# First blocks in halves, u in pairs, another reader first on xm's bank, gate columns inside a z block, first output blocks by token tile

## The chip, the cores and the metric

The kernel runs on one core of a Trainium2 chip. PE is TensorE's matmul, PEld its weight load, DVE is VectorE, ACT is ScalarE, POOL is GpSimd, SP is SyncE, which only issues transfers here. The metric is the device time of one execution in microseconds, the median of several runs.

## The reference

Two layers on x of 256 tokens by 1024. Layer 0 mixes tokens with a gated MLP, layer 1 with an mLSTM; behind each stands a SwiGLU and a gated embedding.

```python
def gmlp_mixer(x, w_in, ln_g, ln_b, w_s, b_s, w_out):
    u, v = jnp.split(jax.nn.gelu(x @ w_in), 2, axis=-1)      # 3072 each
    v = layer_norm(v, ln_g, ln_b)
    sv = jnp.einsum('gts,bcsgd->bctgd', jnp.tril(w_s), v_in_groups) + b_s
    return (u * sv) @ w_out

def mlstm_mixer(x, ...):
    xm, z = jnp.split(x @ w_in, 2, axis=-1)                  # 2048 each
    xc = silu(causal_depthwise_conv(xm, conv_w, conv_b))     # 4 taps
    q, k, v = headwise_linear(xc, w_q), headwise_linear(xc, w_k), headwise_linear(xm, w_v)
    gates = concatenate([q, k, v]) @ w_gates + b_gates       # 4 heads, i and f
    h = mlstm_cell(q, k, v, i_pre, f_pre)                    # chunkwise, stabilised
    h = layer_norm(h, norm_g) + skip * xc
    return (h * silu(z)) @ w_out

def swiglu(x, w_gate, w_up, w_down):
    return (silu(x @ w_gate) * (x @ w_up)) @ w_down

for i in range(2):
    x = layer_norm(ALPHA * x + mixer_i(x), ln1_g[i], ln1_b[i])
    x = layer_norm(ALPHA * x + swiglu(x, ...), ln2_g[i], ln2_b[i])
    x = x + sigmoid(x @ ple_w_gate[i] + ple_b_gate[i]) * (p[i] @ ple_w_proj[i])
```

## The kernel before

All products are made in float32 out of two float32r parts: an operand is split into a high part (a cast, by ACT) and a low part (the difference, by DVE), and a product takes three matmuls: high by high, high by low, low by high. The weights come from memory as blocks of 128 by 1024 (512 KB, tile `raw`, four buffers) in the order of a plan, and `split` makes `w` of them. `ahead(loads, casts)` issues the loads of the next blocks on SP's queue and the splits of the next few; `weight(...)` calls it at each use. A raw buffer is free again when DVE has subtracted, and the next load waits for that. `EARLY` moves some blocks of a later stage up in the plan. The Tile scheduler sets the order of each engine's instructions from the order of the code and its own estimates; semaphores follow from the data.

The stages on PE, in the order of time:

- warm-up matmuls, then the six v columns (`vps`): tokens on the output's partitions, four blocks of weights each. x comes in four pieces of two K blocks (`xr`), the first of them as two transfers of ACT's queue; the first weight block comes and is split in halves of 512 columns (`HALF`), all others whole.
- the u blocks (`ups`, features on the partitions, 24 matmuls of 256 tokens), each followed by the spatial products (`svps`, `sv_block`) and, three blocks later, by the output matmuls (`acc`, 12 of 512). `us` is the Gelu of the bank.
- layer 0's SwiGLU, where g and u go in pairs: `feat_pair` multiplies the high weights by both parts of x at once (8 matmuls of 512 columns into two halves of one bank), then the low weights by the high part (8 of 256), and `pair_sum` adds the two halves (a copy by ACT, an addition by DVE).
- layer 1: z's first 512 features, then sixteen xm blocks (`xm_block`: the convolution from the bank, split of xm, Silu, split of xc), the q and v blocks two blocks later (`qv_block`, `qps`, `vps`), the scores a block after that (`s_block`), and z blocks 4 to 7 in between (`z_mm`).
- the gates: `gp` transposes the gate sums, DVE and ACT make the cumulative sums (`ai`, `G`, `ex`), `cp` transposes them back to columns, `gb` broadcasts G to all partitions for each head. z blocks 8 to 11 lie between.
- the heads: `pv_block(h)` makes `num` and `pd`, and a chain of small DVE and POOL operations gives the scale `hrs` and the offset `nb` with which ACT writes `hn`; then a z block each; `h_block(h)` transposes `hn` and makes four input blocks `h` of the output product.
- the output blocks `mo` (`Down.add`, tokens 0 to 127, then 128 to 255), layer 1's SwiGLU and embedding.

PSUM has eight banks, four of kind A (gp, cp, gb, num, acc) and four of kind B (vps, ups, svps, zps, tp, pg, pu); a tile waits for the readers of the bank's earlier tile.

Of the kernel before, what the change touches and what calls it, by code (L numbers as in the profile page):

```python
# [14 lines left out]
P = 128  # L15
D = 1024
S = 256
# [51 lines left out]
def paired(key):  # L69

    return key[0] in ("g", "u") and len(key) == 3 and key[-1] >= 4

# [60 lines left out]
def trunk(ctx, tc, a, out):  # L133
# [35 lines left out]
    def ahead(loads, casts):  # L169
        while at["load"] < min(len(plan), at["use"] + loads):  # L170
            ap = plan[at["load"]][1]
            n = ap.shape[-1]
            t = tl("raw", [P, n], name="raw")
            for c in HALF if at["load"] == 0 else [slice(0, n)]:
                sp.dma_start(t[:, c], ap[:, c])
            raws[at["load"]] = t
            at["load"] += 1
        while at["cast"] < min(len(plan), at["use"] + casts):
            i = at["cast"]
            key, raw = plan[i][0], raws.pop(i)  # L180
            n = raw.shape[-1]
            if key in WIDE:
                t = tl("b8", [P, 2, D], F32R, "w")
            else:


                first = ASIDE if stationary(key) and not paired(key) else 0
# [12 lines left out]
            wt[i] = t  # L200
            at["cast"] += 1
# [44 lines left out]

    def feat_from_x(ps, w):

        for k in range(KD):
            mm_feat(ps, w, slice(k * P, (k + 1) * P), xh[:, k, :], xl[:, k, :], k == 0, k == KD - 1)  # L250

# [96 lines left out]
    for i in range(4):  # L348
        t = tl("m2", [P, 2, S], name="xr")
        if i == 0:  # L350
            for k in range(2):
                act.dma_start(t[:, k, :], a["xT"][i, :, k, :])
        else:
            sp.dma_start(t, a["xT"][i])
        ahead(1 + i, int(i == 0))
        xr.append(t)
    make_identity(nc, ident)
# [288 lines left out]
    def mlstm(embed1):  # L646
# [41 lines left out]

        def z_mm(f):
            ps = bank("B", [P, S], "zps")  # L690
            feat_from_x(ps, weight("z", f, casts=2 if f > 10 else None))
            return f, ps
# [9 lines left out]
        def xm_block(f):  # L702
            ps = bank("B", [P, S], "xmps")
            feat_from_x(ps, weight("xm", f))
            y = tl("s", [P, S], name="conv")
            act.activation(y, ps, AF.Identity, bias=par[:, f, 4:5], scale=par[:, f, 3:4])
            for j in (1, 2, 3):
                dve.scalar_tensor_tensor(y[:, j:], ps[:, :S - j], par[:, f, 3 - j:4 - j], y[:, j:], ALU.mult, ALU.add)
# [85 lines left out]
        with tc.manual_schedule(engines={mybir.EngineType.Activation}):  # L794
            z8 = z_mm(8)
            gp = bank("A", [4, 2, S], "gp")
            for i in range(2):
                for t in range(2):
                    pe.transpose(gp[:, i, TOK[t]], gacc[:, t, 4 * i:4 * i + 4], ident)
            dve.tensor_scalar(fs, gp[:, 1, :], gbias[:, 1:2], None, ALU.add)  # L800
# [9 lines left out]
            z_copy(*z8)  # L810
            z = z_mm(9)
            cp = bank("A", [P, 4, 4], "cp")
            for i, src in enumerate((ai, ex)):
                for t in range(2):
                    pe.transpose(cp[:, 2 * i + t, :], src[:, TOK[t]], ident[:4, :4])
            dve.tensor_copy(cols[:, 0:2, :], cp[:, 0:2, :])

            dve.tensor_scalar(cols[:, 2:4, :], cp[:, 2:4, :], -88.0, None, ALU.max)
            for h in range(NH):
                gb = bank("A", [P, 2, P], "gb")  # L820
                pe.matmul(gb, selH[:, h, :], G, start=True, stop=True)
                if h in (0, 3):
                    z_copy(*z)
                    z = z_mm(10 if h == 0 else 11)
                gm = tl("s", [P, 2, P], name="gm")
# [13 lines left out]
            z_copy(*z)  # L839
            act.activation(sz[1][:, 0:4, :], sz[1][:, 0:4, :], AF.Silu)  # L840

        hn = []

        def pv_block(h):
# [18 lines left out]
            dve.tensor_tensor(dn, dn, pd[:, :, 0], ALU.max)  # L863
            dve.reciprocal(dn, dn)
            st = tl("c", [P, 2, 6], name="hst")
            mv = tl("c", [P, 2, 2], name="hmv")
# [137 lines left out]
```

## Time and profile before

| | us |
|---|---|
| median of 3 runs (837.59, 838.34, 840.28) | 838.34 |
| profiled execution | 837.17 |
| span of the profile | 835.4 |
| PE, DVE, ACT, POOL busy | 824.1, 608.8, 472.5, 158.4 |

The span is from the first to the last instruction on the core; the execution's time has 1.8 us more around it. The granted clock was 0.999. An engine's idle time counts only where PE ends up waiting for it.

### The profile page before, as it was taken

What the parts mean: (1) busy time and instruction counts of PE and PEld (TensorE: products, weight loads), DVE (VectorE), ACT (ScalarE), POOL (GpSimd) and SP (SyncE); (2) the same over time, 40 slices, a digit from 0 to 9 for tenths busy, and PEclk for the clock granted to TensorE, in tenths of its full rate; (3) what the DMA queues carried; (4) which work ended last, traced back from release to release, by engine and by line L of the source; (5) the groups of instructions that cost most, each with busy time, mean ns of one, the idle gap of its engine ahead of it and who ended that gap; (6) DMA issues with size and microseconds to landing.
All of it is one profiled execution on the core that took longest, in us unless ns stands there. A gap on an engine that the chain in (4) does not pass through costs nothing.

```text
span 835.4 us, 12743 instructions
## 1 busy us (share of the span) xinstructions
PE 824.1 (99%) x4727; PEld 719.6 (86%) x4727; DVE 608.8 (73%) x933; ACT 472.5 (57%) x803; POOL 158.4 (19%) x222
## 2 busy tenths in 40 slices
PE   8999999999999999999999999999999999999997
PEld 5889999998888888888889999898878888888886
DVE  6667996567856666578878998578886666677684
ACT  6556665555544555467347787685544555566522
POOL 1021654443100001800101655230010000000010
PEclk9999999999999999999999999999999999999999
DMA  8885465567286655588234444253646655577601
GB/s 299 294 304 178 143 196 192 177 196 243 102 290 202 188 191 193 164 261 265 80 134 165 140 140 154 95 193 121 209 166 243 206 190 193 187 244 259 202 0 52
DMA packets 44710, 155.55 MB, mean 186 GB/s; under 512 B 5224, under 2 KB 5992, under 8 KB 44648
## 3 DMA queue, kind: packets, MB, share of 16 engines
q1 hardware_dynamic: 44360, 154.47, 56.0%
q8 instruction: 37, 0.61, 0.3%
q10 hardware_dynamic: 288, 0.26, 0.1%
q14 instruction: 25, 0.20, 0.1%
HBM read 153.67 MB, written 1.05 MB: 185 GB/s over the span
## 4 chain that ended last, share of the span: by engine, by line
PE 63%; DVE 5%; DMA 3%; ACT 2%; issue 1%; POOL 1%; DVEq 0%; ACTq 0%; SPq 0%; POOLq 0%
PE pu L255 8%; PE pg L255 8%; PE acc L239 5%; PE acc L238 5%; PE acc L240 5%; PE pu L257 4%; PE pg L257 4%; PE gate L275 2%; PE gate L278 2%; PE gate L276 2%; PE first L275 2%; PE first L278 2%; PE first L276 2%; DVE w L152 2%; DMA raw<-in_ml_wo 1%; PE xmps L243 1%
## 5 line engine op out<-in xcount | busy, mean ns | idle before, releaser
L152 DVE TENSOR_TENSOR w<-raw,w 128x1024 fp32r<-128x1024 f32 (+1 forms) x277 | 337.2, 1225 | 108.6 <-ACT w L152 106.0
L152 ACT CAST w<-raw 128x1024 fp32r<-128x1024 f32 (+1 forms) x276 | 287.3, 1045 | 152.7 <-PE acc L240 50.7
L238 PE MATMUL acc<-w,h 128*128 128x512 f32 x336 | 132.0, 393 | 1.6 <-ACT hn L878 1.0
L239 PE MATMUL acc<-w,h 128*128 128x512 f32 x336 | 131.5, 391 | 0.0
L240 PE MATMUL acc<-w,h 128*128 128x512 f32 x336 | 130.8, 390 | 0.5 <-DVE w L152 0.5
L238 PEld LDWEIGHTS acc<-w,h 128*128 128x128 f32 x336 | 63.2, 188 | 14.5 <-ACT hn L878 1.4
L240 PEld LDWEIGHTS acc<-w,h 128*128 128x128 f32 x336 | 63.1, 188 | 14.5 <-DVE w L152 1.0
L239 PEld LDWEIGHTS acc<-w,h 128*128 128x128 f32 x336 | 63.2, 188 | 11.1 <-DVE h L152 0.3
L255 PE MATMUL pu<-xs,w 128*128 128x512 f32 x288 | 72.3, 393 | 0.0
L255 PE MATMUL pg<-xs,w 128*128 128x512 f32 x288 | 71.8, 391 | 0.0
L255 PEld LDWEIGHTS pg<-xs,w 128*128 128x128 f32 x288 | 53.8, 188 | 11.0
L307 POOL TENSOR_SCALAR ve<-mv 128x1 f32<-128x1 f32 x8 | 6.1, 758 | 294.8 <-DVE mv L327 290.5
L255 PEld LDWEIGHTS pu<-xs,w 128*128 128x128 f32 x288 | 51.5, 188 | 9.3
L244 PE MATMUL ups<-xs,w 128*128 128x256 f32 x192 | 53.7, 280 | 0.0
L243 PE MATMUL ups<-xs,w 128*128 128x256 f32 x192 | 53.6, 279 | 0.0
L245 PE MATMUL ups<-xs,w 128*128 128x256 f32 x192 | 53.6, 279 | 0.0
L442 POOL TENSOR_TENSOR sv<-sv,cf 128x256 f32<-128x256 f32 x24 | 31.1, 1298 | 67.8 <-ACT sv L441 64.0
L257 PEld LDWEIGHTS pg<-xs,w 128*128 128x128 f32 x288 | 38.9, 188 | 3.1
L257 PEld LDWEIGHTS pu<-xs,w 128*128 128x128 f32 x288 | 38.9, 188 | 3.1
L257 PE MATMUL pu<-xs,w 128*128 128x256 f32 x288 | 39.5, 279 | 0.0
L257 PE MATMUL pg<-xs,w 128*128 128x256 f32 x288 | 39.4, 279 | 0.0
L238 PE MATMUL vps<-w,xs 128*128 128x512 f32 x96 | 37.6, 392 | 1.5 <-ACT w L152 0.8
(240 smaller groups left out, 1675.7 us busy)
## 6 DMA issues: line engine op xcount, KB each, us to landing
raw<-in_ffn_g SPq DMA_DIRECT2D x44, 512.0 KB, 3.9
raw<-in_ffn_u SPq DMA_DIRECT2D x44, 512.0 KB, 4.0
raw<-in_ffn_d SPq DMA_DIRECT2D x44, 512.0 KB, 3.4
raw<-in_gm_u SPq DMA_DIRECT2D x24, 512.0 KB, 3.5
raw<-in_gm_wo SPq DMA_DIRECT2D x24, 512.0 KB, 3.4
raw<-in_gm_v SPq DMA_DIRECT2D x23, 512.0 KB, 4.9
raw<-in_ple_gate SPq DMA_DIRECT2D x16, 512.0 KB, 4.5
raw<-in_ml_z SPq DMA_DIRECT2D x16, 512.0 KB, 3.3
```

Source lines behind the costliest of these rows:

```text
L152: return dve.tensor_copy(hi, src) if fast else act.copy(hi, src), sub.tensor_tensor(lo, src, hi.bitcast(F32), ALU.subtract)
L238: pe.matmul(ps, lh, w[:, 0, c], start=start, stop=False)
L239: pe.matmul(ps, ll, w[:, 0, c], start=False, stop=False)
L240: pe.matmul(ps, lh, w[:, 1, c], start=False, stop=stop)
L243: pe.matmul(ps, w[:, 0, c], h, start=start, stop=False)
L244: pe.matmul(ps, w[:, 0, c], l, start=False, stop=False)
L245: pe.matmul(ps, w[:, 1, c], h, start=False, stop=stop)
L255: pe.matmul(ps, w[:, 0, k * P:(k + 1) * P], xs[:, k], start=k == 0, stop=False)
L257: pe.matmul(ps[:, 0], w[:, 1, k * P:(k + 1) * P], xh[:, k, :], start=False, stop=k == KD - 1)
L275: pe.matmul(ps, xh[:, k, TOK[t]], w[:, 0, c], start=k == 0, stop=False)
L276: pe.matmul(ps, xh[:, k, TOK[t]], w[:, 1, c], start=False, stop=False)
L278: pe.matmul(ps, xl[:, k, TOK[t]], w[:, 0, c], start=False, stop=k == KD - 1)
```

## The change

Eight edits: one more warm-up matmul; the first three weight blocks in halves, with the second piece of x on SP's queue between the first two halves; `ple_gate`'s first six blocks three steps earlier in the plan; the u blocks in pairs; the split of xm ahead of the three convolution steps; the gate transposes inside z8, the column transposes and all of G's broadcasts (now two per bank) inside z10, and z12 ahead of head 0; head h's scale by other operations; four splits ahead of head 3, no z block behind it, and the first two output blocks by token tile.

```diff
-WARM = 7
+WARM = 8
+GATES_STEP = 3
-EARLY |= {("d", l, 13 + k): ("pg", l, k) for l in range(2) for k in range(6)}
+EARLY |= {("d", l, 10 + k): ("pg", l, k) for l in range(2) for k in range(6)}
...
-            for c in HALF if at["load"] == 0 else [slice(0, n)]:
+            for c in HALF if at["load"] < 3 else [slice(0, n)]:
                 sp.dma_start(t[:, c], ap[:, c])
+                if at["load"] == 0 and c.start == 0:
+                    second_x()
...
-                for c in () if key[0] == "bdv" else HALF if i == 0 else [slice(0, n)]:
+                for c in () if key[0] == "bdv" else HALF if i < 3 else [slice(0, n)]:
                     split(t[:, 0, c], t[:, 1, c], raw[:, c], fast=i == 0 and c.start == 0)
...
     def u_block(f):
-        ps = bank("B", [P, S], "ups")
-        feat_from_x(ps, weight("u", f))
+        ps = bank("B", [P, 2, S], "ups")
+        feat_pair(ps, weight("u", f))
         us[f] = tl("s", [P, S], name="u")
-        act.activation(us[f], ps, AF.Gelu_apprx_tanh)
+        pair_sum(us[f], ps)
+        act.activation(us[f], us[f], AF.Gelu_apprx_tanh)
...
-            act.activation(y, ps, AF.Identity, bias=par[:, f, 4:5], scale=par[:, f, 3:4])
-            for j in (1, 2, 3):
-                dve.scalar_tensor_tensor(y[:, j:], ps[:, :S - j], par[:, f, 3 - j:4 - j], y[:, j:], ALU.mult, ALU.add)
...
+            act.activation(y, ps, AF.Identity, bias=par[:, f, 4:5], scale=par[:, f, 3:4])
             split(xm[0][:, 0, :], xm[0][:, 1, :], ps)
+            for j in (1, 2, 3):
+                dve.scalar_tensor_tensor(y[:, j:], ps[:, :S - j], par[:, f, 3 - j:4 - j], y[:, j:], ALU.mult, ALU.add)
...
-            z8 = z_mm(8)
             gp = bank("A", [4, 2, S], "gp")
...
+            z8 = z_mm(8, (GATES_STEP, transpose_gates))
...
-            z = z_mm(9)
+            z_copy(*z_mm(9))
...
+            gbs = [bank("A", [P, 2, 2, P], "gb") for _ in range(2)]
+            z = z_mm(10, (GATES_STEP, transpose_cols))
...
-            act.activation(sz[1][:, 0:4, :], sz[1][:, 0:4, :], AF.Silu)
+            z_copy(*z_mm(12))
+            act.activation(sz[1][:, 0:5, :], sz[1][:, 0:5, :], AF.Silu)
...
-            dve.tensor_tensor(rs, mv[:, :, 1], dn, ALU.mult)
-            dve.tensor_tensor(rs, rs, dn, ALU.mult)
-            rsqrt(rs, rs, 2)
+            for t in range(2):
+                dve.tensor_scalar(rs[:, t:t + 1], mv[:, t, 1:2], dn2[:, t:t + 1], EPS, ALU.mult, ALU.add)
+            pool.tensor_tensor(rs, rs, mhalf[:, :2], ALU.pow)
...
         for h in range(NH):
+            if h == NH - 1:
+                ahead(LOAD_AHEAD, 4)
             pv_block(h)
-            z_act(*z_mm(12 + h))
+            if h < NH - 1:
+                z_act(*z_mm(13 + h))
...
-                acc.add(f, hs.pop(f), weight("mo", f, casts=1 if f >= NI - 2 else None))
+                block = (f, hs.pop(f), weight("mo", f, casts=1 if f >= NI - 2 else None))
+                if f == 0:
+                    first = block
+                elif f == 1:
+
+                    for t in range(2):
+                        for b, h2, w in (first, block):
+                            acc.mm(b, t, h2, w)
+                else:
+                    acc.add(*block)
```

`between` is a pair of a K step and a function that `feat_from_x` calls ahead of that step, so `GATES_STEP = 3` puts the transposes behind 9 of a z block's 24 matmuls. `second_x` issues the transfer of x's second K block.

How the instructions stand on DVE at the start: the low parts of x and of the first weight blocks, before,

```order
L152 CAST w<-raw 128x512
L152 TENSOR_TENSOR xs<-xr,xs 128x256
L152 TENSOR_TENSOR w<-raw,w 128x512
L152 TENSOR_TENSOR xs<-xr,xs 128x256
L152 TENSOR_TENSOR w<-raw,w 128x512
L152 TENSOR_TENSOR xs<-xr,xs 128x2x256
L152 TENSOR_TENSOR w<-raw,w 128x1024
L152 TENSOR_TENSOR xs<-xr,xs 128x2x256
L152 TENSOR_TENSOR w<-raw,w 128x1024
```

and with the change (line 152 is line 153 now):

```order
L153 CAST w<-raw 128x512
L153 TENSOR_TENSOR xs<-xr,xs 128x256
L153 TENSOR_TENSOR w<-raw,w 128x512
L153 TENSOR_TENSOR xs<-xr,xs 128x256
L153 TENSOR_TENSOR w<-raw,w 128x512
L153 TENSOR_TENSOR xs<-xr,xs 128x2x256
L153 TENSOR_TENSOR w<-raw,w 128x512 x2
L153 TENSOR_TENSOR xs<-xr,xs 128x2x256
L153 TENSOR_TENSOR w<-raw,w 128x512 x2
```

The second and third weight block are two subtractions each.

ACT in one xm block late in layer 1's projection (`conv` is the convolution, `vsum` the v product, `q` the query), before,

```order
L706 ACTIVATE conv<-xmps,par 128x256
L735 COPY vsum<-vps 128x136
L152 CAST w<-raw 128x4x128
L735 COPY vsum<-vps 128x136
L152 CAST vn<-vsum 128x2x128
L152 CAST xm<-xmps 128x256
L715 ACTIVATE conv<-conv 128x256
L152 CAST xm<-conv 128x256
L152 CAST q<-qps 128x256
```

and with the change:

```order
L721 ACTIVATE conv<-xmps,par 128x256
L153 CAST xm<-xmps 128x256
L745 COPY vsum<-vps 128x136 x2
L153 CAST w<-raw 128x4x128
L153 CAST vn<-vsum 128x2x128
L725 ACTIVATE conv<-conv 128x256
L153 CAST xm<-conv 128x256
L153 CAST q<-qps 128x256
```

The cast of xm moved from behind the v product's copies to directly behind the convolution's first step; the q cast stays last.

DVE from the end of head 1 to the start of head 2 (`dn` and `hrs` are the scale of a head, `w<-raw,w` the subtraction of a weight block), before,

```order
L868 BN_STATS hst<-num 128x6
L869 BN_AGGR hmv<-hst 128x2
L871 TENSOR_TENSOR hrs<-hmv,dn 128x2
L872 TENSOR_TENSOR hrs<-hrs,dn 128x2
L874 TENSOR_TENSOR hrs<-hrs,dn 128x2
L876 SCALAR_TENSOR_TENSOR nb<-hmv,hrs 128x2
L862 SCALAR_TENSOR_TENSOR dn<-pd,cols 128x2
```

and with the change:

```order
L890 BN_STATS hst<-num 128x6 x2
L891 BN_AGGR hmv<-hst 128x2 x2
L894 TENSOR_SCALAR hrs<-hmv,dn_5791 128x1 x2
L153 TENSOR_TENSOR w<-raw,w 128x1024
L896 TENSOR_TENSOR hrs<-hrs,dn 128x2
L898 SCALAR_TENSOR_TENSOR nb<-hmv,hrs 128x2
L153 TENSOR_TENSOR w<-raw,w 128x1024
L882 SCALAR_TENSOR_TENSOR dn<-pd,cols 128x2
```

Two subtractions of weight blocks now stand between the heads, where before none stood; before, the next one came behind the first of the output blocks' inputs of head 1.

More of the change, by code (lines that the diff above doesn't have):

```diff
@@ L69, in paired @@
 def paired(key):
-    return key[0] in ("g", "u") and len(key) == 3 and key[-1] >= 4
+    return key[0] in ("g", "u") and len(key) == 3 and key[-1] >= 4 or key[0] == "u" and len(key) == 2
 def weight_plan(a):
@@ L245, in mm_feat, with feat_from_x @@
         pe.matmul(ps, w[:, 1, c], h, start=False, stop=stop)
-    def feat_from_x(ps, w):
+    def feat_from_x(ps, w, between=(None, None)):
         for k in range(KD):
+            if k == between[0]:
+                between[1]()
             mm_feat(ps, w, slice(k * P, (k + 1) * P), xh[:, k, :], xl[:, k, :], k == 0, k == KD - 1)
@@ L350, in trunk @@
         if i == 0:
-            for k in range(2):
-                act.dma_start(t[:, k, :], a["xT"][i, :, k, :])
+            act.dma_start(t[:, 0, :], a["xT"][i, :, 0, :])
+            second_x = lambda: sp.dma_start(xr[0][:, 1, :], a["xT"][0, :, 1, :])
+            xr.append(t)
         else:
             sp.dma_start(t, a["xT"][i])
+            xr.append(t)
         ahead(1 + i, int(i == 0))
-        xr.append(t)
     make_identity(nc, ident)
@@ L687, in transpose_z, with z_mm @@
                 act.copy(sz[0][:, 0:4, TOK[t]], tp)
-        def z_mm(f):
+        def z_mm(f, between=(None, None)):
             ps = bank("B", [P, S], "zps")
-            feat_from_x(ps, weight("z", f, casts=2 if f > 10 else None))
+            feat_from_x(ps, weight("z", f, casts=2 if f > 10 else None), between)
             return f, ps
@@ L794, in mlstm, with transpose_gates @@
         with tc.manual_schedule(engines={mybir.EngineType.Activation}):
-            z8 = z_mm(8)
             gp = bank("A", [4, 2, S], "gp")
-            for i in range(2):
-                for t in range(2):
-                    pe.transpose(gp[:, i, TOK[t]], gacc[:, t, 4 * i:4 * i + 4], ident)
+            def transpose_gates():
+                for i in range(2):
+                    for t in range(2):
+                        pe.transpose(gp[:, i, TOK[t]], gacc[:, t, 4 * i:4 * i + 4], ident)
+            z8 = z_mm(8, (GATES_STEP, transpose_gates))
             dve.tensor_scalar(fs, gp[:, 1, :], gbias[:, 1:2], None, ALU.add)
@@ L810, in mlstm, with transpose_cols @@
             z_copy(*z8)
-            z = z_mm(9)
+            z_copy(*z_mm(9))
             cp = bank("A", [P, 4, 4], "cp")
-            for i, src in enumerate((ai, ex)):
-                for t in range(2):
-                    pe.transpose(cp[:, 2 * i + t, :], src[:, TOK[t]], ident[:4, :4])
+            def transpose_cols():
+                for i, src in enumerate((ai, ex)):
+                    for t in range(2):
+                        pe.transpose(cp[:, 2 * i + t, :], src[:, TOK[t]], ident[:4, :4])
+                for h in range(NH):
+                    pe.matmul(gbs[h // 2][:, h % 2], selH[:, h, :], G, start=True, stop=True)
+            gbs = [bank("A", [P, 2, 2, P], "gb") for _ in range(2)]
+            z = z_mm(10, (GATES_STEP, transpose_cols))
             dve.tensor_copy(cols[:, 0:2, :], cp[:, 0:2, :])
@@ L819, in mlstm @@
             for h in range(NH):
-                gb = bank("A", [P, 2, P], "gb")
-                pe.matmul(gb, selH[:, h, :], G, start=True, stop=True)
-                if h in (0, 3):
+                gb = gbs[h // 2][:, h % 2]
+                if h == 3:
                     z_copy(*z)
-                    z = z_mm(10 if h == 0 else 11)
+                    z = z_mm(11)
                 gm = tl("s", [P, 2, P], name="gm")
@@ L870, in pv_block @@
             rs = tl("c", [P, 2], name="hrs")
-            dve.tensor_tensor(rs, mv[:, :, 1], dn, ALU.mult)
-            dve.tensor_tensor(rs, rs, dn, ALU.mult)
-            rsqrt(rs, rs, 2)
+            for t in range(2):
+                dve.tensor_scalar(rs[:, t:t + 1], mv[:, t, 1:2], dn2[:, t:t + 1], EPS, ALU.mult, ALU.add)
+            pool.tensor_tensor(rs, rs, mhalf[:, :2], ALU.pow)
             dve.tensor_tensor(rs, rs, dn, ALU.mult)
```

3 lines of the change are left out of this document (added).

## The prediction

> **What bounds the kernel now.** First the page's busy times and the waits of TensorE (PE), the second with its columns engine, line, what it waited for, total, times, longest:
>
> ```profile
> PE 824.1 (99%) x4727; PEld 719.6 (86%) x4727; DVE 608.8 (73%) x933; ACT 472.5 (57%) x803; POOL 158.4 (19%) x222
> ...
> PE qps L243 <- DVE q L152: 1.5, 1, 1.5
> ...
> PE acc L238 <- ACT hn L878: 1.0, 1, 1.0
> PE vps L238 <- ACT w L152: 0.8, 1, 0.8
> ...
> PE acc L240 <- DVE w L152: 0.5, 1, 0.5
> ```
>
> PE is busy for 824.1 of 835.4 us. So the end moves by only two things: fewer PE cycles, or fewer of its waits, each of which happens once. No other engine bounds the whole; but one does so for a stretch. Busy time by stretch (columns after the sum: PE, weight loads, DVE, ACT, POOL, clock, DMA share, GB/s):
>
> ```profile
> 79.00:115.00 36.00, 35.94 (x261) 33.75 (x261) 35.10 (x53) 23.99 (x45) 18.59 (x18) 1.00 0.46 147
> 115.00:208.00 93.00, 93.00 (x610) 84.95 (x609) 63.24 (x84) 50.47 (x82) 41.53 (x47) 1.00 0.63 203
> ...
> 552.00:575.00 23.00, 21.95 (x145) 19.62 (x145) 16.66 (x59) 18.26 (x31) 5.75 (x10) 1.00 0.13 45
> ```
>
> From 79 to 115 us DVE (VectorE) works 35.10 of 36.00 us, and PE keeps pace with nothing to spare; from 115 to 208 it has 29.8 us free. The third row is used below. The granted clock is 1.00 throughout, so no gain or loss comes from there.
>
> **The start (halves).** PE and the engines that feed it, in order of time (start, duration; in brackets the idle time before and its releaser):
>
> ```profile
> 6.21 0.69 DVE L152 TENSOR_TENSOR w<-raw,w 128x512 fp32r<-128x512 f32 x1
> ...
> 7.92 0.62 PE L240 MATMUL vps<-w,xs 128*128 128x512 f32 x2
> 8.29 1.04 ACT L152 CAST w<-raw 128x1024 fp32r<-128x1024 f32 x1 [1.58 <-DMA raw<-in_gm_v]
> ...
> 9.38 0.50 PE L238 MATMUL vps<-w,xs 128*128 128x512 f32 x1 [0.83 <-ACT w L152]
> ...
> 9.72 0.40 PE L239 MATMUL vps<-w,xs 128*128 128x512 f32 x1
> ...
> 10.19 0.40 PE L239 MATMUL vps<-w,xs 128*128 128x512 f32 x1
> 10.23 1.05 ACT L152 CAST w<-raw 128x1024 fp32r<-128x1024 f32 x1 [0.38 <-DMA raw<-in_gm_v]
> ...
> 10.64 0.73 PE L240 MATMUL vps<-w,xs 128*128 128x512 f32 x2
> ```
>
> A 512-wide matmul follows the one before it by 0.23 us (9.72 to 10.19 holds two). After the pair at 7.92 the next was due at 8.38; it came at 9.38 (1.00 lost), the restart cost another 0.11 (9.38 to 9.72), and 10.19 to 10.64 with its restart another 0.22 + 0.11: 1.44 in all. The cause: the second v block is cast whole, 1.04 us on ACT, after it has landed whole at 8.29. In halves: between the casts at 8.29 and 10.23 a block and an x piece land, 768 KB in 1.94 us, so half a block (256 KB) is an estimated 0.65 us and the first half lands near 7.65. Its cast takes, like the 512-wide DVE row, some 0.65: ready 8.3, before PE's 8.38. Its low part takes 0.69 more: 9.0, against 8.83 for the third matmul, 0.15 left. The second half is ready in time. Price: one more transfer on SP's queue for each of the two blocks, the second x piece moved to that queue, and 0.15 us more DVE work a block (2 x 0.69 against 1.23 for a whole one). I take -1.3; ends -0.7 (the first half 0.6 later through the queue, an estimate by one half's own 0.65) and -1.5 (the whole of it and more). The eighth warm-up matmul ends before the first v data and is priced at nothing.
>
> **u in pairs.** A u block is 24 matmuls of 256 now; the FFN's pg and pu already go as 8 of 512 and 8 of 256:
>
> ```profile
> 149.44 0.28 PE L243 MATMUL ups<-xs,w 128*128 128x256 f32 x1
> ...
> 152.23 0.64 PE L435 MATMUL svps<-ws,vn 128*128 128x256 f32 x4
> ...
> 301.47 1.98 PE L255 MATMUL pg<-xs,w 128*128 128x512 f32 x8
> ...
> 304.23 2.01 PE L255 MATMUL pu<-xs,w 128*128 128x512 f32 x8
> ...
> 307.01 0.40 PE L238 MATMUL acc<-w,h 128*128 128x512 f32 x1
> ```
>
> Unpaired: 152.23 - 149.44 = 2.79. Paired behind an acc block: 2.76; paired behind a paired one: 2.78. As means over all such blocks of the trace they are 2.798, 2.754 and 2.780. u blocks stand behind acc blocks in 21 of 24 cases, so 21 x 0.044 + 3 x 0.02 = 1.0 us off; lower end 24 x 0.018 = 0.4. The Trainium skill, "TensorE: Matmul & The Clock Gate", section "Back-to-back issue gap", puts the gap at N/2.4 + 2.5 ns: 24 x 109.2 = 2.62 us against 8 x 215.8 + 8 x 109.2 = 2.60. By it the gain would be 24 x 0.02 = 0.5 us and the sum 0.5 higher; this trace's pitches are longer (0.117 and 0.227), and I keep them.
>
> What it costs: per block a copy on ACT and an add on DVE, and the bank is held until the add instead of until the Gelu. DVE's row for the same add:
>
> ```profile
> L261 DVE TENSOR_TENSOR y<-y,pu 128x256 f32<-128x256 f32 x36 | 15.1, 420 | 16.9 <-ACT y L260 16.9
> ```
>
> 24 x 0.42 = 10.1 us of DVE work. From 115 us on, 29.8 free us cover the 16 adds there (6.7). Between 79 and 115, about 8 blocks add 3.4 us where 0.9 is free: 2.5 must come from somewhere. PE (35.94 of 36.00) showed one wait there, so all the other hand-overs from DVE had some slack, and one had none:
>
> ```profile
> 91.27 0.48 DVE L443 SCALAR_TENSOR_TENSOR sv<-svps,gmp,sv 128x256 f32<-128x256 f32 x1 [0.64 <-POOL sv L442]
> ...
> 91.80 0.74 PE L435 MATMUL svps<-ws,vn 128*128 128x256 f32 x4
> ```
>
> svps started as DVE's row had read the bank. So the loss lies between -0.3 (that wait goes) and +2.5 (all of it shows on PE); behind slack that was not used, most of it drains after 115. I take +0.4.
>
> **ACT reads xm's bank first.** ACT's cast of xm stands behind DVE's three convolution steps on the same bank:
>
> ```profile
> ACT xm L152 <- DVE conv L708: 8.0, 7, 2.4
> ...
> 522.36 1.21 DVE L152 TENSOR_TENSOR w<-raw,w 128x1024 fp32r<-128x1024 f32 x1
> ...
> 523.50 0.47 DVE L708 SCALAR_TENSOR_TENSOR conv<-xmps,par,conv 128x253 f32<-128x253 f32 x1
> ...
> 524.00 0.37 ACT L152 CAST xm<-xmps 128x256 fp32r<-128x256 f32 x1 [2.25 <-DVE conv L708]
> ...
> 525.19 0.37 ACT L152 CAST q<-qps 128x256 fp32r<-128x256 f32 x1
> ...
> 526.13 0.39 PE L243 MATMUL qps<-xm,bdm 128*128 128x256 f32 x1 [1.45 <-DVE q L152]
> ```
>
> ACT stood 2.25 us behind a DVE weight subtraction that had slipped between two convolution steps; behind ACT, the q cast came at 525.19, DVE's q after it, and PE lost 1.6 us start to start (the wait of 1.5 in the list). Afterwards ACT casts directly behind its own conv step. Queued behind that now are DVE's subtraction (0.41) and three convolutions, so Silu comes 0.4 later; PE reads its result two blocks on, some 10 us later, which covers it. I take -1.5: nearly all of that loss. Ends -0.6 (ACT's 2.25 go, and DVE's weight subtraction of 1.2 still lies in the way) and -2.0 (some tenths from shorter waits of the same kind, of which ACT's row counts seven). The Trainium skill, "PSUM — Partial Sum Buffer", section "PSUM bank collisions raise a hardware error", says that two engines may not touch one bank at once, reads included. The 8.0 us of waits agree: the readers go in turn, the change picks the turn and removes none.
>
> **Gates and head blocks.** gp is transposed after 9 of z8's 24 matmuls, so DVE's chain starts 15 x 0.117 = 1.75 us earlier; the transposes of the columns and G's broadcasts stand together within z10.
>
> ```profile
> 529.86 0.33 PE L243 MATMUL zps<-xs,w 128*128 128x256 f32 x1
> ...
> 538.26 0.28 PE L815 MATMUL cp<-ident,gt 4*128 4x4 f32 x2 [0.27 <-DVE gt L806]
> ...
> 544.90 0.72 PE L857 MATMUL pd<-ones,sc 128*128 128x2 f32 x6
> ```
>
> From 529.86 to 544.90 PE needs 15.04 us for four z blocks of 2.80 and about 2.4 of transposes and broadcasts, 13.6. The rest, 1.4, is the wait for the chain and restarts at each change of operand. Afterwards there are fewer restarts; but the transposes now come together, and their last two need the chain's end, which from the row of 538.26 on (the first two, freed by L806) still takes a scan and an addition, 1.1 us; PE reaches them 0.5 us before that by the earlier start. So half goes: -0.7 (0 to -1.4). The POOL addition that leaves the head chain, and the small DVE operations that replace it, lie under PE's matmuls.
>
> **First output blocks.** With the last z block ahead of head 3, its matmuls no longer lie between head 3 and the first output; instead token tile 0 of four blocks comes first.
>
> ```profile
> 565.00 0.50 PE L857 MATMUL pd<-ones,sc 128*128 128x2 f32 x4
> ...
> 572.09 0.39 PE L239 MATMUL acc<-w,h 128*128 128x512 f32 x1
> 573.47 0.50 PE L238 MATMUL acc<-w,h 128*128 128x512 f32 x1 [0.99 <-ACT hn L878]
> ```
>
> PE lost 1.15 + 0.11 here: tile 1's banks are held until ACT has written hn of head 3. Head 3's chain took 8.0 us from its last matmuls (to 565.5) to the restart. Now PE has the transposes (0.8), 24 matmuls (5.5), transposes again (0.8) and one matmul: 7.3 us of work ahead of that point, against 6.9 before. So some 0.8 of the wait stays: -0.3, ends -1.2 (the shorter chain) and +1.0 (DVE does head 0's outputs ahead of it).
>
> **The late output weights.**
>
> ```profile
> 573.86 1.22 DVE L152 TENSOR_TENSOR w<-raw,w 128x1024 fp32r<-128x1024 f32 x1
> ...
> SPq L175 <- DVE w L152: 60.1, 23, 22.5
> ...
> 608.37 1.05 ACT L152 CAST w<-raw 128x1024 fp32r<-128x1024 f32 x1 [1.17 <-DMA raw<-in_ml_wo]
> ...
> 610.73 0.50 PE L240 MATMUL acc<-w,h 128*128 128x512 f32 x1 [0.53 <-DVE w L152]
> ```
>
> DVE did no weight for some 22 us up to 573.86; the raw buffers stayed full, SP's queue waited 22.5 us, DMA was at 0.13 (third stretch above), and at 608 the last output block came late: 0.50 + 0.70 and a restart, 1.3 us. Now three of DVE's subtractions stand earlier, so three loads start earlier, some 6 us at 512 KB per 2 us. I take -1.3, ends -1.4 and 0. The gate weights three blocks earlier change no listed wait: 0.
>
> **Sum.** -1.3 - 1.0 + 0.4 - 1.5 - 0.7 - 0.3 - 1.3 = -5.7. The profiled execution took 837.17, so 831.5; the median of the runs shown, 838.34, stands 1.17 above it: **832.6**, own range 831.0 to 834.2.
>
> **The rivals.**
> - All terms at their better ends (-1.5, -1.0, -0.3, -2.0, -1.4, -1.2, -1.4: -8.8) are too much together; two thirds of the step beyond the forecast give -7.8, 830.5. For it: most terms are waits with a known end. Chance 0.08.
> - DVE becomes the bound from 79 to 115 us, and its 2.5 us show on PE as waits of ups or svps: 832.6 - 0.4 + 2.5 = 834.7 (833.7 to 836.3). For it: 35.10 of 36. Against: PE waited 0.06 us there so far, so the other hand-overs have slack. Chance 0.22.
> - The change does not do what it says: the loads come no earlier, neither the halves nor the output weights, because the DMA share between 575 and 608 is already 0.7 and each half costs an issue. +1.3 and +1.3: 835.2. Chance 0.12.
> - Slower: the pair's add becomes the release of every u bank, and PE waits for one add (0.42 us) in each of 24 blocks: -0.4 + 10.1 on 832.6 is 842.3. It decides when the add comes later than the bank's next use, some 6 us after its matmuls. Against: pg and pu use their banks the same way and no wait of theirs is in the list. Chance 0.06.
> - The sum as it stands: 0.52.
>
> **How the numbers follow.** A change of 0.3% (2.5 us) is about what a measurement here can tell from none: faster is below 835.8. The sum and the better ends are faster (0.60); of the DVE case 0.14, of the DMA case 0.06: 0.80. Same: 0.08 + 0.06 = 0.14. Slower 0.06. The range 829.8 to 836.2 leaves out the slower case and the tails.
>
> **What would show it.** Right: the waits of vps for ACT w, qps for DVE q and acc for w gone from PE's list; PE at about 818 busy; u blocks of 2.75. Wrong: new waits of ups or svps for DVE between 79 and 115, a wait for hn above 1.2, or ACT's wait for conv moved to another reader of the bank that PE then waits for.

## The result, and the profile after

The changed kernel takes 834.1 us (median of five executions, 833.62 to 835.45) against 838.37 of the kernel before: a ratio of 0.9946, 95% interval 0.9927 to 0.9965. Forecast were 832.6 and a gain of 5.7; 4.3 came. The profiled execution took 833.62 with a span of 831.8.

Executions of one kernel differ here by their mean granted clock, 0.993 to 1.000, and that difference turned out to be half of the story; it is told below with its numbers.

The page of the kernel after, and PE's waits:

```profile
PE 822.8 (99%) x4536; PEld 711.9 (86%) x4536; DVE 620.3 (75%) x963; ACT 481.3 (58%) x827; POOL 161.9 (19%) x218
...
PE warm L352 <- DVE warm L349: 1.2, 1, 1.2
PE qps L246 <- DVE q L153: 1.0, 1, 1.0
PE s L767 <- POOL q L753: 0.7, 1, 0.7
PE vps L241 <- DVE w L153: 0.6, 1, 0.6
PE tp L321 <- DVE xn L339: 0.6, 1, 0.6
PE cp L830 <- DVE gt L821: 0.3, 1, 0.3
```

Gone are vps for ACT's w, acc for hn, acc for h and for the late output weights. New is the wait of the transposes of x (`tp`) for DVE's xn; the scores (`s`) wait 0.7 us for POOL's q where they waited 0.2 before; qps for DVE's q has become shorter only. PE's busy time fell by 1.3 us and not to the 818 that were forecast, although 192 u matmuls are fewer. The start times of PE's first matmuls of each stage show where:

| stage on PE, from first matmul to first matmul | before | after | difference |
|---|---|---|---|
| start of the core to v | 5.01 | 5.18 | +0.17 |
| v to u | 68.33 | 67.03 | -1.30 |
| u to the first product of p | 145.79 | 143.91 | -1.88 |
| SwiGLU and embedding of layer 0 | 214.59 | 214.50 | -0.09 |
| z's first block | 11.78 | 11.78 | 0.00 |
| xm to the last score | 84.24 | 84.34 | +0.10 |
| gates and heads to the first output | 39.31 | 39.96 | +0.65 |
| outputs to layer 1's product of p | 48.17 | 45.68 | -2.49 |
| boundary to the first gate product | 3.63 | 4.61 | +0.98 |
| the rest, to PE's last matmul | 210.01 | 210.17 | +0.16 |

Three rows lost what was forecast: the xm stage, the gates, the boundary. The gates first, by stretch (after the sum: PE, weight loads, DVE, ACT, POOL, clock, DMA share, GB/s):

```profile
533.60:537.00 3.40, 3.12 (x18) 2.39 (x18) 3.37 (x7) 3.38 (x4) 0.00 (x0) 0.96 0.12 25
537.00:540.40 3.40, 3.40 (x18) 3.40 (x18) 3.23 (x7) 1.72 (x5) 0.00 (x0) 0.54 0.88 270
540.40:543.80 3.40, 3.40 (x31) 3.40 (x31) 3.00 (x3) 3.00 (x7) 1.64 (x1) 1.00 0.97 343
```

In the second stretch PE is busy for all of 3.40 us and does 18 matmuls where the undisturbed one behind it holds 31: the granted clock was 0.54 (laid exactly, it was 0.50 from 536.70 to 540.11, and 1.00 before and behind). The matmuls of z10 start 0.213 us apart there instead of 0.117, 14 of them, 1.35 us lost, 1.5 with the ones at the edges. It follows the column transposes, their wait of 0.39 and the eight broadcast matmuls (two passes for each of four broadcasts), together 2.6 us of PE in which only 4 of 128 rows hold data. Scattered, as before, they had not done it in the profiled execution.

The xm stage, where the forecast took the wait of qps away (POOL, DVE and PE, in order of time):

```profile
520.13 2.26 POOL L153 TENSOR_TENSOR vn<-vsum,vn 128x256 fp32r<-128x256 f32 x1
520.26 1.21 DVE L153 TENSOR_TENSOR w<-raw,w 128x1024 fp32r<-128x1024 f32 x1
521.40 0.41 DVE L153 TENSOR_TENSOR xm<-conv,xm 128x256 fp32r<-128x256 f32 x1
521.74 0.41 DVE L153 TENSOR_TENSOR q<-qps,q 128x256 fp32r<-128x256 f32 x1
522.20 0.38 PE L246 MATMUL qps<-xm,bdm 128*128 128x256 f32 x1 [1.03 <-DVE q L153]
522.38 0.92 POOL L728 TENSOR_SCALAR a<-conv,par 128x256 f32<-128x256 f32 x1
...
523.26 0.46 POOL L753 CAST q<-wx 128x16 fp32r<-128x16 f32 x3
523.50 0.39 PE L767 MATMUL s<-q,xm 128*128 128x264 f32 x1 [0.69 <-POOL q L753]
```

ACT is early now, but DVE's q stands behind the same weight subtraction (520.26), so qps still waits 1.0. And POOL's subtraction for vn took 2.26 us instead of 0.74; behind it stand POOL's small copies into q, and the scores wait for them. One wait was shortened by 0.4 us start to start, another grew to 0.85.

The boundary, ACT, DVE and PE:

```profile
606.73 1.05 ACT L153 CAST w<-raw 128x1024 fp32r<-128x1024 f32 x1 [2.56 <-DMA raw<-in_ple_proj]
...
607.81 1.23 DVE L153 TENSOR_TENSOR w<-raw,w 128x1024 fp32r<-128x1024 f32 x1 [2.38 <-ACT w L153]
608.95 1.28 DVE L330 SCALAR_TENSOR_TENSOR xn<-xn,acc 128x512 f32<-128x512 f32 x2
...
614.48 0.63 PE L321 MATMUL tp<-ident,xn 128*128 128x128 f32 x4 [0.58 <-DVE xn L339]
```

The weight block of ple_proj landed late, its subtraction stands ahead of the normalisation on DVE, and DVE waited 2.38 us for it with the normalisation behind. Of the 2.49 us that the output blocks gained, this execution gave one back.

### The profile page after: what moved, and what is told of

Its sections match the earlier page's. It is cut to its first block, busy times and chain, and to the rows that moved or that the text cites. A ratio compares the mean times of both kernels' runs of the same rounds, so it can differ in the third digit from the quotient of the medians.

```text
span 831.8 us, 12438 instructions
## 1 busy us (share of the span) xinstructions
PE 822.8 (99%) x4536; PEld 711.9 (86%) x4536; DVE 620.3 (75%) x963; ACT 481.3 (58%) x827; POOL 161.9 (19%) x218
## 3 DMA queue, kind: packets, MB, share of 16 engines
HBM read 153.67 MB, written 1.05 MB: 186 GB/s over the span
## 4 chain that ended last, share of the span: by engine, by line
PE 87%; issue 5%; DVE 5%; POOL 1%; ACT 1%; DMA 0%; DVEq 0%; POOLq 0%
PE pu L261 8%; PE pg L261 8%; PE acc L242 8%; PE acc L241 8%; PE acc L243 7%; PE ups L261 5%; PE pu L263 4%; PE pg L263 4%; PE ups L263 3%; PE vps L243 3%; PE vps L241 3%; PE vps L242 3%; PE gate L281 2%; PE gate L284 2%; PE first L282 2%
## 5 line engine op out<-in xcount | busy, mean ns | idle before, releaser
L261 PE MATMUL ups<-xs,w 128*128 128x512 f32 x192 | 47.7, 391 | 0.0
L261 PEld LDWEIGHTS ups<-xs,w 128*128 128x128 f32 x192 | 35.7, 188 | 7.2
L266 ACT COPY s<-pg 128x256 f32<-128x256 f32 x36 | 13.4, 373 | 48.2 <-PE pg L263 48.2
L451 POOL TENSOR_TENSOR sv<-sv,cf 128x256 f32<-128x256 f32 x24 | 23.8, 992 | 73.0 <-ACT sv L450 69.2
```

The source lines that it names most:

```text
L261: pe.matmul(ps, w[:, 0, k * P:(k + 1) * P], xs[:, k], start=k == 0, stop=False)
L266: act.copy(o, ps[:, 1])
L451: pool.tensor_tensor(sv, sv, cf.unsqueeze(1).to_broadcast([P, 2, P]), ALU.add)
```

## The experiments

Two theories stood against each other for each loss. All stage times are PE's, from the profile of each run; the single executions among them are compared by stage, since whole times differ by the clock.

**G's broadcasts laid apart.** Each behind three matmuls of z10 instead of in one piece:

```diff
-                for h in range(NH):
-                    pe.matmul(gbs[h // 2][:, h % 2], selH[:, h, :], G, start=True, stop=True)
+            z = z_mm(10, {3: transpose_cols} | {4 + h: broadcast(h) for h in range(NH)})
```

> The changed kernel, with G's four broadcasts (4 partitions wide) laid one by one between the steps of z10 instead of in one piece of 1.9 us behind the column transposes. Theory A, few-row matmuls in one piece make the throttle halve PE's clock: no stretch of half clock behind them (it was 3.4 us long, 16 matmuls at 0.213 us instead of 0.117), mean clock back from 0.997 to 0.999, and from the last score matmul to the first output matmul 38.3 to 38.6 us instead of 39.96. Theory B, it is the restart after the wait for the transposes that does it: the half clock stays, 39.9 us or more, since four more restarts of 0.1 us come in.

The clock was 0.995, and the stage took 42.94 us: worse, not better. The granted clock was 0.50 from 540.27 to 547.10, twice as long as in the first profile of the changed kernel, and 1.00 before it. Laid three matmuls apart, the broadcasts fill 4.8 us instead of 1.9, and the last of them ran at half clock. Theory A's remedy failed; the time is as theory B has it (39.9 or more), but a half clock of twice the length it did not foresee.

**The same broadcasts on 128 rows.**

```diff
-        gt = tl("row", [4, 4, S], name="gt")
+        gtw = tl("row", [P, 4, S], name="gt")
+        gt = gtw[:4]
...
-                    pe.matmul(gbs[h // 2][:, h % 2], selH[:, h, :], G, start=True, stop=True)
+                    pe.matmul(gbs[h // 2][:, h % 2], selw[:, h * P:(h + 1) * P], gtw[:, 3, :], start=True, stop=True)
```

> The changed kernel, with G and its selectors padded by zeros to 128 partitions, so that the same broadcasts at the same place and of the same length use all 128 rows of the array; the column transposes stay 4 rows wide. Theory A, the rows in use count: no half clock, 38.4 us from the last score matmul to the first output matmul instead of 39.96. Theory B, the wait ahead of them or their number counts: half clock as in the changed kernel, 39.9 us. A third, that zeros count as idle rows: also 39.9 us.

38.45 us, clock 0.999, as theory A says: the granted clock is 1.00 up to 829 us. (The broadcasts follow one another by 0.216 us here, as in the changed kernel ahead of its half clock; that is their own pitch, 0.117 that of the z blocks' matmuls.) But five of the six profiles below with the gates as changed had no half clock there either (38.4 to 38.8 us). One execution does not settle it.

**xm's split behind the convolution again.**

> The changed kernel with the three convolution steps ahead of xm's split again, as before. Theory A, the new order gains nothing because the wait on the bank was replaced by waits for POOL and for DVE's weight subtraction: the xm stage (first xm matmul to last score matmul) takes 84.2 to 84.6 us, as the 84.34 with the change and 84.24 before. Theory B, the new order does gain its 1.5 us and something else of the change took them: 85.5 us or more.

83.96 us: as long as POOL makes the copies into q, the new order gains nothing, theory A. This run has qps waiting 1.4 for DVE's q and no wait of the scores for POOL. The records of POOL say why. Its sixteen subtractions for vn overlap a weight subtraction of DVE in 7 cases in the kernel before, in 14 with the change, and in 7 with the old order put back; without overlap each took 0.73 to 0.75 us, with 0.47 us of overlap 1.07, with 0.98 1.59, with 1.21 1.82 and once 2.26. By line, before and after, 440 to 530 us:

```profile
L152 POOL TENSOR_TENSOR vn<-vsum,vn 128x256 fp32r<-128x256 f32 x16 | 12.8, 802 | 1.8 <-ACT vn L152 0.9
```

```profile
L153 POOL TENSOR_TENSOR vn<-vsum,vn 128x256 fp32r<-128x256 f32 x16 | 19.8, 1239 | 1.4 <-ACT vn L153 0.4
```

The Trainium skill, "SBUF — State Buffer", section "SBUF: two separate sides", says that DVE and POOL share a pair of ports, held by one of them for a whole instruction, for DVE operations with two inputs too. The trace agrees: where DVE was first or within 0.02 us of it, POOL's time is 0.6 us and the overlap; where POOL was first by 0.1 us, it took 0.74, and DVE's weight subtraction 1.7 instead of 1.21. The 2.26 us of the row at 520.13 look like an exception, since POOL starts 0.13 ahead of the weight subtraction there; but a copy of DVE ran from 519.93, and it, the weight subtraction and that of xm follow one another to 521.81: 1.67 us from POOL's start, and 0.6.

**Layer 1's gate blocks later.**

```diff
-EARLY |= {("mo", 8 + 2 * k): ("g", 1, k) for k in range(4)}
+EARLY |= {("mo", 8 + 2 * k): ("g", 1, k) for k in range(2)}
```

> The changed kernel with two instead of four of layer 1's gate blocks loaded between the output weights. Theory A, the wait for the first transposes of x at the boundary (0.6 us, 0.99 start to start) comes from ple_proj's block, which lands late behind those loads and stands ahead of the normalisation on DVE: the boundary (first product of p to first gate product) falls from 4.61 to 3.6 us, the wait of tp for DVE xn is gone, and the end comes 0.9 to 1.1 us earlier, if the gate blocks loaded later are still in time. Theory B, the boundary is bound by DVE's own chain: 4.5 us and more, nothing gained.

The boundary fell to 3.61 us, as in theory A, though the wait for DVE's xn did not go, it came behind it; and the first gate products took 25.99 us instead of the 23.04 of the changed kernel's second profile. Of these 2.95, 0.82 is that wait for xn and 0.92 one for a delayed block; the rest is restarts and a wait of 0.19:

```profile
621.13 0.63 PE L321 MATMUL tp<-ident,xn 128*128 128x128 f32 x4 [0.82 <-DVE xn L339]
...
629.05 0.74 PE L281 MATMUL first<-w,xs 128*128 128x512 f32 x2 [0.92 <-ACT w L153]
```

And the boundary takes 3.61 to 3.81 us in every other run, the changed kernel's second one included. So the loss of 0.98 belongs to that execution and not to the four loads; the edit is no remedy. (This execution also had the clock at half twice, from 525.06 and from 538.71 us.)

**u unpaired again.**

> The changed kernel with the u blocks unpaired (24 matmuls of 256, Gelu from the bank) as before. Theory A, the pairs are worth their fewer matmul starts and the waits that they happened to remove: from the first u matmul to the first product of p 145.3 to 145.8 us instead of 143.91, the last block's wait for h (0.8 us before, 0.35 with the change) back. Theory B, most of the 1.9 us that this stage gained came from elsewhere: 144.4 or less.

144.96 us, 1.05 more than in the first profile of the changed kernel: between the two theories' bounds, and the size that the prediction gave the pairs. It is one execution, and this stage of the paired kernels went from 143.6 to 144.9 in the other runs, so the sign and not the tenth is shown. Theory A has the size of it, but its last sign failed: the last block's wait for h did not come back. The rows divide the stage's 1.88 as follows. The u blocks' own pitches give 0.96 (18 of them stand behind acc blocks and went from 2.798 to 2.754 us); the wait of svps, which is back here, and its restart 0.3; and 0.6 is shorter waits of acc, mostly the last block's for h. That last part is not the pairs': unpaired too, this run has no such wait, and what took it was not traced.

**Second and third block whole again.**

> The changed kernel with the second and third v block loaded and split whole again (the second x piece stays on SP's queue). Theory A, the halves remove the wait for the second block: without them the first v matmul to the first u matmul takes 68.2 to 68.5 us instead of 67.03. Theory B, it was x's piece on the other queue: 67.0 to 67.3.

68.35 us, 1.32 more: theory A. The wait of vps for ACT's w is back at 0.9. (Here the clock was at half from 524.78 to 528.20 us, behind the waits of qps and of the scores.)

**The old order of the heads and outputs.**

> The changed kernel with the old order of the heads: z12 to z15 one behind each head, no four splits ahead of head 3, the output blocks one by one. Theory A, this part lets the output weights come earlier and takes the wait for hn away: without it, from the first output matmul to the first product of p 47.8 to 48.3 us instead of 45.68, and the boundary behind it 3.6 instead of 4.61. Theory B, the shorter chain of small operations alone took the wait for hn: 46.8 or less.

45.94 us, and acc waits 0.2 us for hn: theory B. The output weights were not late either, which neither theory had. DVE's weight subtractions, of which none had stood between 551 and 573.8 us before, stand at 553, 557, 563 and 571 us here, though the heads' order is the old one (with the new order at 556, 559 and 573). So the new order of the heads did not bring the weights in time. The gates inside the z blocks and the heads' shorter chain are what this run keeps of the edits there; which of them let DVE come to the weights sooner was not tested. Gates to first output are 38.70 us, 0.3 more than the undisturbed 38.4 with the new order. The new order of heads and outputs is worth about half a microsecond.

**The small copies into q on ACT.**

```diff
-            pool.tensor_copy(q[:, :, S:], wx[:, NI + f, :].rearrange("p (i n) -> p i n", i=2))
+            act.copy(q[:, :, S:], wx[:, NI + f, :].rearrange("p (i n) -> p i n", i=2))
```

> The changed kernel with the sixteen small copies into q on ACT instead of POOL. Theory A, the wait of the scores for POOL (0.85 us start to start near the end of the xm stage) is POOL's queue, where the low part of vn took 1.8 to 2.3 us: gone, and the xm stage takes 83.3 to 83.6 us instead of 84.34. Theory B, the scores are then held by DVE's q instead: 84.1 or more.

83.12 us and no wait of the scores: theory A. With the copies off POOL, the stage is 1.12 shorter than before the change. How much of that is the order of xm's readers is open, since the old order was not run with the copies on ACT; with them on POOL it had no wait for POOL and took 83.96.

**The changed kernel once more.**

> The changed kernel once more, for the spread of its clock and time. Theory A, the throttle looks at PE in windows whose phase is free, and the 3 us of few-row matmuls and waiting in z10 fill one in some executions and not in others: executions with a mean clock of 0.997 or less beside others of 0.999 and more, the former some 1.5 us longer. Theory B, the clock fell in the five executions of the first measurement because the code always makes it fall, and the four kernels that kept 1.0 did so for their edits: all five at 0.998 or less. The ratio to the kernel before between 0.9927 and 0.9965 again.

Eleven executions: 834.67 us, 831.28 to 838.1, ratio 0.994 (0.992 to 0.996). Seven had a clock of 0.993 to 0.996, three 0.998, one 1.000, which took 831.28. The kernel before, 22 executions beside them: seven at 0.999 or 1.000 (836.9 to 838.16, median 837.2), fifteen at 0.994 to 0.997 (837.55 to 843.14). So the clock falls in both kernels, in some executions, and theory A holds for its being free; it was never only the gates. The profiled one of the eleven had it in another place, the xm stage:

```profile
462.00:467.00 5.00, 3.05 (x26) 2.85 (x26) 5.00 (x11) 3.35 (x9) 4.31 (x7) 1.00 0.45 150
467.00:471.00 4.00, 4.00 (x24) 4.00 (x23) 2.09 (x3) 0.74 (x2) 2.95 (x3) 0.57 0.33 122
```

There the scores had waited 1.95 us for POOL (its vn took 2.55 us, its `a` 2.94), and behind that wait 15 matmuls ran at half clock; the granted clock was 0.50 from 467.37 to 470.78. A wait of 1.95 us cost 1.45 more. The gates stage of this execution was undisturbed: 38.8 us.

**The q copies on ACT, timed.**

> The changed kernel with the sixteen small copies into q on ACT instead of POOL, timed. If POOL's queue held the scores, 1.0 to 1.5 us less than the changed kernel, ratio to it about 0.9985; the clock as in the changed kernel, since the gates are the same.

830.67 us (829.37 to 831.5, six executions), ratio to the kernel before 0.9892 (0.9868 to 0.9916), against 0.994 for the changed kernel beside it: 4.0 us less, where 1.0 to 1.5 were expected. The wait is 1.35 of it (82.99 us in the xm stage); the rest is the clock: three executions at 1.000, three at 0.998, none lower. The expectation that the clock would be as before was wrong: the half clock behind POOL's wait goes with the wait, and only the gates are left to bring one. PE's waits:

```profile
PE warm L352 <- DVE warm L349: 1.2, 1, 1.2
PE qps L246 <- DVE q L153: 1.0, 1, 1.0
PE cp L830 <- DVE gt L821: 0.3, 1, 0.3
PE vps L241 <- DVE w L153: 0.3, 1, 0.3
```

**Columns and broadcasts on 128 rows, with q on ACT.** As above, and the columns as products of the padded rows with the identity.

> The same with G, its selectors and the gate columns padded by zeros to 128 partitions: column transposes (as products with the identity) and broadcasts use all rows of the array. Theory A, few rows in use make the window count as idle: no execution below 0.999 of clock, and no pitch of 0.213 us in the profile; 0 to 1.5 us less than with 4 rows. Theory B, it is the wait or the change of shapes: the clock falls as often as with 4 rows.

All six executions at 0.999 or 1.000, as theory A says, and the profile grants the full clock up to 830 us. But 832.06 us (831.31 to 832.95), 1.4 more than with 4 rows: this build has waits that the 4-row one has not, the scores for DVE's q (1.1) and the embedding's products for ACT's xs (0.8), the latter ahead of anything that was edited. Both stand in the profile of the broadcasts on 128 rows too, with 0.7 and 0.2. Why the order shifted there was not traced.

**The broadcasts twice.**

```diff
+                    for _ in range(2):
                         pe.matmul(gbs[h // 2][:, h % 2], selH[:, h, :], G, start=True, stop=True)
```

> The changed kernel with each of G's broadcasts issued twice (4 rows, 3.8 us instead of 1.9). Theory A: the stretch of few rows is now about 4.5 us, longer than the 3.4 us of low clock seen so far, so every execution shows half clock, 0.997 or less, and it costs 1.9 us of matmuls and 1.5 us of clock more than an undisturbed execution: about 834.5. Theory B: as the changed kernel plus 1.9.

Ten executions, none above 0.998, eight of them at 0.992 to 0.996 with 836.1 to 839.55; the median of 837.18 is 2.5 us more than that of the changed kernel beside it, of which 1.9 are the matmuls. One kept 0.998, where theory A had every execution at 0.997 or less, but it is nearer than theory B; the profile has it where theory A puts it, and a second one in the xm stage (523.98 to 527.39 us):

```profile
536.00:540.00 4.00, 3.73 (x21) 3.17 (x20) 3.97 (x8) 3.97 (x6) 0.00 (x0) 1.00 0.36 114
540.00:544.40 4.40, 4.40 (x24) 4.11 (x23) 4.02 (x7) 3.07 (x9) 2.03 (x1) 0.62 0.91 291
```

## Why the prediction was right, point by point

The sign, the range and most of the sizes held; that the sum came within 1.5 us is in part luck, as its steps show:

- **Start, -1.3.** Measured -1.30 in the stage and +1.32 when the halves were undone. The first v matmul came 0.17 later in this execution.
- **Pairs, -1.0.** 0.96 by the blocks' own pitches: 2.754 us for a paired u block behind an acc block, as forecast (18 blocks stand so, not 21; it changes the sum by less than 0.1). 1.05 came back when they were undone, with the spread given above; that spread alone would not tell the trace's pitches from the 0.5 of the Trainium skill's formula, which its section gives for a matmul by itself.
- **DVE from 79 to 115 us, +0.4.** Mis-sized: nothing was lost, and svps's wait went (the better end, -0.3). DVE had 34.73 busy of the same 36.00 us, PE 36.00:

```profile
77.90:113.90 36.00, 36.00 (x203) 31.39 (x202) 34.73 (x55) 25.47 (x50) 16.64 (x18) 1.00 0.47 147
```

DVE does 11 weight subtractions there instead of 12, with the additions of the pairs in between. That the splits run ahead of their use and the additions ate into that lead is argued from this count, not tested.
- **xm, -1.5.** This step failed: +0.10 in the stage, and the old order gives 83.96, 0.38 less. The step's own quoted rows had the reason: DVE's weight subtraction of 1.21 between two convolution steps. The prediction freed ACT from it and left q's subtraction on DVE behind it; and it priced nothing on POOL, whose operations now fall beside DVE's: that made a wait of 0.85. It cost clock too: of the nine profiles with the new order and the copies on POOL, four have a half clock in this stage (85.7 to 87.7 us); the five with the old order or the copies on ACT have none.
- **Gates and heads, -0.7.** Right where the clock holds: 38.4 against 39.31 is -0.9. In the profiled execution +0.65, since 1.5 us went to the clock. The sentence that failed is "no gain or loss comes from there": it read the mean of 0.999 of one execution as a property of the kernel.
- **First outputs and late weights, -0.3 and -1.3.** -2.49: both waits went whole. For the weights the mechanism was the named one, DVE's subtractions standing earlier; but the four splits ahead of head 3 were not needed for it. Of hn, 0.8 were expected to stay; nothing did (0.2 with the old order of heads and outputs).
- **A new wait behind the gain.** The boundary's 0.98 was no term of the sum; it was there in one of the changed kernel's two profiled executions, with the late landing of ple_proj's block.
- **The signs.** Of those named for being right, the waits of vps for ACT's w and of acc for w went and the u blocks came to 2.75 us; qps for DVE's q stayed at 1.0, and PE is busy for 822.8 and not some 818. The 818 does not follow from the sum: only the pairs and some restarts take busy time away, the other terms are waits, and half clock adds some 1.5.

Between executions at full clock the change is worth -5.9 (837.2 to 831.28, the latter a single one), against the forecast of -5.7. So the sum came out for a kernel at full clock by luck, by errors that cancelled: the xm step was 1.6 too good, the u stage with its DVE term 1.3 and the outputs 0.9 too bad. The shortfall of the medians, 4.3 for 5.7, goes with the clock: among 22 executions of the kernel before 7 kept it, among 16 of the changed kernel one. (Five of the kernel before at 0.997 took 837.74 in the median, only 0.5 more than those at full clock, so a half clock does not cost the same everywhere.)

## What to carry to other kernels

When a wait stands behind two engines, taking one out of the way is worth only what the other leaves: follow the other's queue to the instruction that releases, and look at POOL's operations beside DVE's before moving either. Read the mean clock of every execution, not of the profiled one alone: a kernel whose PE is full paid here for a wait of 1.95 us with 1.45 more, and for 2.6 us of products with few rows with 1.5 more, in the executions in which the clock fell. The remedy that paid was to take sixteen copies (0.41 us each on POOL in the first profile, 0.22 on ACT) off the engine that had become late, not to rearrange the products.

## What the hardware showed that was not expected

- PE's granted clock halves for 3.41 us behind a stretch in which PE waits or multiplies with 4 rows, once for two such lengths in a row, in some executions of the same program and not in others: 1.3 to 1.7 us lost for each single one. By their times, executions of the changed kernel at 1.000 (831.3), 0.996 (about 834.7) and 0.993 to 0.994 (836 to 838) look like none, two, and three or more of them (3.41 us at half take 0.002 off the mean); only the profiled ones were seen. The Trainium skill, "TensorE: Matmul & The Clock Gate", section "Part 1: The HAM clock gate", tells of free-running windows of 3.4 us that set the clock to half or full; the lengths here and the change from execution to execution agree. Its table has the clock fall after an idle window; here PE was never idle for a whole one.
- What counts, rows or time, can be worked out from the traces. Lay a grid of 3.41 us over each of the fourteen, from its first record of the clock (4.2 to 6.6 us; every fall lies on this grid), and add up the matmuls in each stretch, at 0.117 us for 256 columns, the z blocks' pitch. These are the eight stretches ahead of a fall and, of those at full clock from there to the last 8 us, the two lowest without one:

| profile | 3.41 us from | 128 rows, us | 4 rows, us | clock behind it |
|---|---|---|---|---|
| layer 1's gate blocks later | 535.30 | 0.61 | 0.94 | 0.50 |
| broadcasts twice | 537.63 | 0.66 | 1.38 | 0.50 |
| changed kernel, first | 533.28 | 0.72 | 0.94 | 0.50 |
| broadcasts laid apart | 536.86 | 0.95 | 0.70 | 0.50 |
| layer 1's gate blocks later | 521.65 | 1.19 | 0 | 0.50 |
| second and third block whole | 521.37 | 1.22 | 0 | 0.50 |
| broadcasts twice | 520.57 | 1.22 | 0 | 0.50 |
| changed kernel, second | 463.96 | 1.30 | 0 | 0.50 |
| broadcasts on 128 rows | 521.88 | 1.41 | 0 | 1.00 |
| second and third block whole | 535.02 | 1.45 | 0.60 | 1.00 |

The sum over 128 rows alone sorts them: no fall follows 1.41 or more, a fall follows each of 1.30 or less, and the one stretch at half clock that held less than that (1.11, broadcasts laid apart) is the one behind which the clock stayed down. The sum of both does not: it reaches 2.03 ahead of a fall, and thirteen stretches without one hold less. So in these traces matmuls with 4 rows did not count as work. The phase of the grid differs from execution to execution. Moved over the trace, it finds 1.35 or less at 0.60 of its phases in the kernel before, at 0.61 with q on ACT, and at none with columns and broadcasts on 128 rows too; below 0.999 were 15 of 22, three of seven, and none of six executions. It does not give the changed kernel's 15 of 16: its variants with u unpaired and with the old heads, whose profiles had no fall, give 0.70, and a single trace does not show how POOL's wait varies. All this is an estimate from one kernel, with 4 rows as the only few-row case.
- A POOL subtraction of 0.73 us took 1.82 beside a DVE weight subtraction of 1.21 us: it stood still for nearly as long as they overlapped, 1.09 us.
